# Six buffered halves of split weights, float32 work in half chunks, and a gate whose copies and silu are queued behind casts

## The chip, the cores and the metric

The kernel runs on one core of one Trainium2 chip. The metric is the device time of one execution in microseconds (us). The engines are TensorE (PE; its loads of weights are listed as PEld), VectorE (DVE), ScalarE (ACT), GpSimd (POOL) and SyncE (SP), which issues the DMA transfers.

## The reference

Two layers of an encoder for 256 positions of width 1024, in float32. Most of the time goes to the last part of the second layer, a mixture of experts:

```python
def moe_swiglu(xn, router, w_gu, w_down):
    logits = (xn @ router).astype(jnp.float32)
    top_v, top_i = lax.top_k(logits, TOP_K)          # 2 of 8
    w = jax.nn.softmax(top_v, axis=-1)
    ...
    for e in range(N_EXPERTS):
        out = out + comb[..., e:e + 1] * swiglu(xn, w_gu[e], w_down[e])
    return out

def swiglu(xn, w_gu, w_down):
    g, u = jnp.split(xn @ w_gu, 2, axis=-1)
    return (jax.nn.silu(g) * u) @ w_down
```

An expert has `w_gu` of 1024 x 7168 and `w_down` of 3584 x 1024. All eight experts' weights are read, 42 MiB each.

## The kernel before

The positions that chose an expert are gathered into at most 128 slots, and the weights stream past them. They come in chunks of 128 x 2048 float32 (1 MiB, one DMA each, issued by SyncE in the order of use). An expert is seven turns `j`. A turn has two chunks of gate weights, two of up weights, and, from the second turn on, the two chunks of down weights that belong to the turn before; the down chunks of the seventh turn follow after the loop.

TensorE does not multiply float32 at full rate here. A chunk is therefore split in two halves of 1024 columns, and each half in two parts: `hi`, a cast by ScalarE to the type float32r (L168), and `lo`, what VectorE's subtraction leaves of the chunk (L169). Four matmuls of a part use the 512 columns of four blocks of 128 rows. The pools `hi` and `lo` have `NPART = 4` buffers of half a chunk each.

Experts are sorted by how many positions chose them. In the positions 0, 1, 3, 5 and 7 of that order (wide) up to 128 slots are used, the activations are split too, and `moving` runs three matmuls per block: hi with hi, lo with hi, hi with lo. In the positions 2, 4 and 6 (narrow, `two` in the code) at most 64 slots are used; `hi` and `lo` of the activations stand side by side in one tile of 128 columns, and `narrow` runs two matmuls per block, one with each part of the weights. The two halves of the sum lie in the two halves of the partitions and are added afterwards. In narrow positions the last up chunk of a turn is not split: TensorE reads it as float32 (L1139), in eight records for the four blocks.

For a narrow turn the program's order is: gate product (`pg`); transposes of the h of the turn before (`to_rows`, L1172, with a cast at L1053 and a subtraction at L1054); up product (`pu`); then `gate`: two copies by ScalarE that swap the halves of `pg` (L1156, L1157), an addition by VectorE (L1158), silu by ScalarE (L1159), and `eh`, VectorE's product of silu and `pu` (L1163); then the two down products of the turn before.

The order on each engine is made ahead of time by a planner, which goes by program order and by its own estimate of when an instruction's operands and buffers are there. Each engine then works strictly in that order. `tc.issue_after(ins)` makes what is written under it come after `ins` on the same engine. `done[0]` is the last cast that `split` has written.

Chunk buffers come from two pools: 11 of the pool `raw`, and "spare" ones of the pool `big`, ten tiles of a chunk's size that also hold the tokens, the accumulator and other large tiles. `RING` says which chunk takes which kind, and `kinds.append(kinds[-(NRAW + 6)])` repeats it: 17 chunk buffers in all. SyncE issues a load when its buffer is free.

Of the kernel before, what the change touches and what calls it, by code (L numbers as in the profile page):

```python
# [25 lines left out]
F32 = mybir.dt.float32  # L26
F32R = mybir.dt.float32r
I32 = mybir.dt.int32
AF = mybir.ActivationFunctionType
# [3 lines left out]
P = 128  # L33
# [6 lines left out]
NE = 8  # L40
# [4 lines left out]
CH = 2048  # L45
# [4 lines left out]
HALF = CAP // 2  # L50
TCKW = dict(schedule_with_timeline_sim=True)
NCKW = dict(dynamic_dma_scratch_size=512)
NRAW = 11
NPART = 4
RING = "rrrrrrrrsssssrrrrrs"
P2_POOL = (0, 2, 4, 6)
NWARM = 10
NAHEAD = 13
# [23 lines left out]
def _build(ctx, tc, io, cap):  # L82
# [3 lines left out]
    rawp = ctx.enter_context(tc.tile_pool(name="rawp", bufs=NRAW))  # L86
# [3 lines left out]
    work = ctx.enter_context(tc.tile_pool(name="work", bufs=2))  # L90
    w2b, w1b = 4, 5
# [6 lines left out]
    V, S, G, PE = nc.vector, nc.scalar, nc.gpsimd, nc.tensor  # L98

    def f32(ap):  # L100
        return ap.bitcast(F32)
# [41 lines left out]
    def load(ap, n=CH, pieces=1, spare=False):  # L143
# [3 lines left out]
            nc.sync.dma_start(raw[:, sl], ap[:, sl])  # L147
        return raw

    done = []  # L150

    def split(raw, n=CH, pieces=2, apart=()):

        cut = (n // 2 + P - 1) // P * P
        parts = []
        for a, b in ((0, cut), (cut, n)):
            if len(parts) in apart:  # L160
                both = rawp.tile([P, CH], F32R, tag="raw", name="apart")
                hi, lo = both[:, :CH // 2], both[:, CH // 2:]
            else:
                hi = hip.tile([P, CH // 2], F32R, tag="hi", name="hi")
                lo = lop.tile([P, CH // 2], F32R, tag="lo", name="lo")
            step = (b - a) * 2 // pieces
            for i in range(0, b - a, step):
                done[:] = (S.copy(hi[:, i:i + step], raw[:, a + i:a + i + step]),  # L168
                           V.tensor_sub(lo[:, i:i + step], raw[:, a + i:a + i + step],  # L169
                                        f32(hi[:, i:i + step])))  # L170
            parts.append((hi, lo))

        def at(a, b):
            hi, lo = parts[a >= cut]
            o = cut if a >= cut else 0
            return hi[:, a - o:b - o], lo[:, a - o:b - o]
        return at

    class Early:
# [11 lines left out]

        def __call__(self, a, b):
            return self.hi[:, a:b], self.lo[:, a:b]

    def raw_tile(name, dt=F32):
        return rawp.tile([P, CH], dt, tag="raw", name=name)

    def raw_pair(name):
        return [raw_tile(name, F32R) for _ in range(2)]
# [355 lines left out]
    for g, w in enumerate(POOL_WINDOWS):  # L555
        left, right = w // 2, w - 1 - w // 2
        G.memset(invc[:, g, :], 1.0 / w)
        for t in list(range(left)) + list(range(T - right, T)):
            n = min(t + right, T - 1) + 1 - max(t - left, 0)
# [142 lines left out]
    ps = None  # L702
    for m in range(KD):
        if m % 2 == 0:
            ps = halves(acc_tile())
# [4 lines left out]
        for hf in range(2):  # L710
            w = split(load(io["ffn_down"][m, hf], half * P), half * P)
# [86 lines left out]
    last = conv31(KD - 1)  # L798
# [5 lines left out]
    ws = early[:2] + ws  # L804
# [134 lines left out]
    def fetch():  # L939
        n, (ap, pieces) = next(source)  # L940
        ahead.append(load(ap, pieces=pieces, spare=kinds[n] == "s"))
        kinds.append(kinds[-(NRAW + 6)])

    for _ in range(NAHEAD):
        fetch()
# [161 lines left out]
    xg = big_tile("xg", F32R)  # L1107
    ht = big_tile("ht", F32R)

    def whole_chunk():  # L1110
        if not ahead:
            fetch()
        return ahead.popleft()

    def chunk(pieces=2):
        return split(whole_chunk(), pieces=pieces)

    def narrow(ps, xs, ws, first, last):

        n = len(xs)  # L1120
        for part in range(2):
            for i, (x, w) in enumerate(zip(xs, ws)):
                ins = PE.matmul(ps, x, w[part], start=first and i == part == 0,  # L1123
                                stop=last and part == 1 and i == n - 1)
        return ins

    def expert(e, g, following):
        nonlocal fn
        py = out_tiles()
        two = e in NARROW  # L1130

        def gate_up(j, gu):
            pz = acc_tile("gu")
            for kh in range(2):
                xs = [xg[:, k * P:(k + 1) * P] for k in range(kh * 4, kh * 4 + 4)]
                if two and gu == kh == 1:
                    w = whole_chunk()
                    for kk in range(4):
                        PE.matmul(pz, f32(xs[kk]), w[:, kk * 512:(kk + 1) * 512],  # L1139
                                  start=False, stop=kk == 3)  # L1140
                    continue
                w = chunk()
                ws = [w(kk * 512, (kk + 1) * 512) for kk in range(4)]
                if two:
                    narrow(pz, xs, ws, kh == 0, kh == 1)
                    continue
                moving(pz, [(xg[:, k * P:(k + 1) * P], xg[:, D + k * P:D + (k + 1) * P])
                            for k in range(kh * 4, kh * 4 + 4)],
                       ws, kh == 0, kh == 1)
            return pz  # L1150

        def gate(pg, pu):
            sg = work.tile([P, 512], F32, tag="w2", name="esg", bufs=w2b)
            if two:

                S.copy(sg[:HALF], pg[HALF:])  # L1156
                S.copy(sg[HALF:], pg[:HALF])  # L1157
                V.tensor_add(sg, sg, pg)  # L1158
                S.activation(sg, sg, AF.Silu, scale=g.cw[:, 1:2])  # L1159
            else:  # L1160
                S.activation(sg, pg, AF.Silu, scale=g.cw[:, 1:2])
            h = work.tile([P, 512], F32, tag="w2", name="eh", bufs=w2b)
            V.scalar_tensor_tensor(h, pu, g.cw[:, 1:2], sg, op0=ALU.mult, op1=ALU.mult)  # L1163
            return h

        def to_rows(j, h):
            pt = tr_tile("ht")
            o = (j % 2) * D
            if two:

                for i in range(4):
                    PE.matmul(pt[:, i * HALF:(i + 1) * HALF], h[:, i * P:(i + 1) * P], both,  # L1172
                              start=True, stop=True)
                return side_by_side(ht[:, o:o + 512], pt[:, :4 * HALF])
            for i in range(4):
                PE.transpose(pt[:, i * P:(i + 1) * P], h[:, i * P:(i + 1) * P], ident)
            S.copy(ht[:, o:o + 512], pt)
            V.tensor_sub(ht[:, o + 512:o + D], pt, f32(ht[:, o:o + 512]))

        def down(j, n):  # L1180
            w = chunk(4 if e == NE - 1 and j == 6 else 2)
            o = (j % 2) * D
            if two:
                return narrow(py[n], [ht[:, o + f * P:o + (f + 1) * P] for f in range(4)],
                              [w(f * 512, (f + 1) * 512) for f in range(4)], j == 0, j == 6)
            return moving(py[n],
                   [(ht[:, o + f * P:o + (f + 1) * P], ht[:, o + 512 + f * P:o + 512 + (f + 1) * P])
                    for f in range(4)],
                   [w(f * 512, (f + 1) * 512) for f in range(4)], j == 0, j == 6)

        def weighted(n):
            src = py[n]
            hi, lo = (work.tile([P, 512], F32R, tag="w2", name=name, bufs=w2b) for name in ("yh", "yl"))
            S.activation(hi, src, AF.Copy, scale=g.cw[:, 0:1])
            done[:] = [V.scalar_tensor_tensor(lo, src, g.cw[:, 0:1], f32(hi),
                                              op0=ALU.mult, op1=ALU.subtract)]
            return hi, lo

        def scatter(n, y, tile=tr_tile):
            for t in range(2):  # L1200
                pz = tile("so")
                PE.matmul(pz, g.oT[:, t * P:(t + 1) * P], y[0], start=True, stop=False)
                PE.matmul(pz, g.oT[:, t * P:(t + 1) * P], y[1], start=False, stop=True)
                a = acc[:, t * D + n * 512:t * D + (n + 1) * 512]
                V.tensor_add(a, a, pz)  # L1205

        h = None
        for j in range(7):
            pg = gate_up(j, 0)
            if j:  # L1210
                to_rows(j - 1, h)
            pu = gate_up(j, 1)
            h = gate(pg, pu)
            if j:
                down(j - 1, 0)
                if j == 6:
                    to_rows(6, h)
                down(j - 1, 1)
            if following is not None and j in (3, 5):
                following.step(j)  # L1220
        if following is not None:
            following.rows()
        else:
            fn = big_tile("fn")
            nc.sync.dma_start(fn[:, :D], io["final_norm"].to_broadcast([P, D]))
        down(6, 0)
        y = weighted(0)
        last = down(6, 1)
# [276 lines left out]
```

## Time and profile before

| what | value |
| --- | --- |
| time, median of 3 runs | 1547.85 us (1547.59 to 1548.0) |
| profiled execution, its own time | 1547.42 us |
| its span, first to last instruction | 1545.7 us |
| experts, from the first gate matmul to the last scatter | 590.7 to 1532 us |
| wide expert, for instance | 943 to 1066 us |
| narrow experts | 832.5 to 943, 1066 to 1177, 1299 to 1408 us |

Times below are us from the start of the span unless marked ns. Everything before 590 us (the first layer, the convolution module and both attentions) is left as it is by the change, as is what follows the experts.

### The profile page before, as it was taken

The page shows a single profiled execution, that of the slowest core. Times are in us where ns is not written, and L with a number is a line of the kernel's source. Part 1 is how long each engine was busy: PE and PEld are TensorE (multiplying, and loading weights), DVE is VectorE, ACT ScalarE, POOL GpSimd, SP SyncE. Part 2 cuts the span into 40 slices and gives each one's busy share as a digit, 9 for nine tenths or more (in the row PEclk, how much of TensorE's full clock was granted, in tenths as well). Part 3 has the DMA queues.
Part 4 walks back from the last instruction along what each step waited for, and adds up shares of the span by engine and source line. Part 5 has one row for each costly group of instructions (what it writes and reads, how often), then busy time and mean ns, then how long its engine had stood idle before and what let it go on. Part 6 is the DMA issues. An engine that isn't in the chain of part 4 may idle for free.

```text
span 1545.7 us, 23643 instructions
## 1 busy us (share of the span) xinstructions
PE 1511.9 (98%) x8558; PEld 1294.3 (84%) x8558; DVE 1298.9 (84%) x1735; ACT 1052.1 (68%) x1381; POOL 148.1 (10%) x230
## 2 busy tenths in 40 slices
PE   8999999999999999999999999999999999999996
PEld 8899999999998998888888768888667888667885
DVE  7876677776898868999999989889889888889897
ACT  6555554455585647777777877777777777777775
POOL 4710100001394210000000000000000000000000
PEclk9999999999999999999999999999999999999998
DMA  9654454336536566998999999998999999999950
GB/s 370 269 191 164 142 186 166 120 113 236 188 134 244 174 264 221 371 377 334 373 366 342 397 422 412 381 375 331 403 402 376 367 361 343 408 392 382 364 191 30
DMA packets 65213, 451.42 MB, mean 292 GB/s; under 512 B 7360, under 2 KB 7488, under 8 KB 12480
## 3 DMA queue, kind: packets, MB, share of 16 engines
q1 hardware_dynamic: 65088, 449.83, 76.6%
q8 instruction: 69, 1.13, 0.3%
q14 instruction: 56, 0.46, 0.1%
HBM read 448.75 MB, written 1.05 MB: 291 GB/s over the span
## 4 chain that ended last, share of the span: by engine, by line
PE 82%; DVE 9%; POOL 3%; issue 3%; ACT 2%; DMA 1%; SPq 0%; DVEq 0%; POOLq 0%; ACTq 0%
PE gu L211 8%; PE gu L212 8%; PE gu L216 8%; PE acc L205 7%; PE acc L203 7%; PE acc L204 7%; DVE lo L169 6%; PE gu L1139 5%; PE gu L1123 4%; PE py L211 4%; PE py L216 4%; PE py L212 4%; PE py L1123 3%; POOL part L779 2%; PE gx L1042 1%
## 5 line engine op out<-in xcount | busy, mean ns | idle before, releaser
L169 DVE TENSOR_TENSOR lo<-raw,hi 128x1024 fp32r<-128x1024 f32 (+3 forms) x573 | 671.6, 1208 | 113.9 <-ACT hi L168 103.6
L168 ACT CAST hi<-raw 128x1024 fp32r<-128x1024 f32 (+3 forms) x573 | 565.4, 1030 | 212.9 <-PE acc L204 89.4
L169 DVE TENSOR_TENSOR lo<-spare,hi 128x1024 fp32r<-128x1024 f32 (+1 forms) x226 | 260.9, 1198 | 24.4 <-ACT hi L168 20.4
L168 ACT CAST hi<-spare 128x1024 fp32r<-128x1024 f32 (+1 forms) x226 | 221.5, 1035 | 23.6 <-PE gu L212 11.7
L211 PE MATMUL gu<-hi,xg 128*128 128x512 f32 x560 | 218.8, 391 | 0.0
L212 PE MATMUL gu<-hi,xg 128*128 128x512 f32 x560 | 218.3, 390 | 0.0
L216 PE MATMUL gu<-lo,xg 128*128 128x512 f32 x560 | 154.2, 391 | 0.6 <-DVE lo L169 0.6
L216 PEld LDWEIGHTS gu<-lo,xg 128*128 128x128 f32 x560 | 104.7, 188 | 23.9 <-DVE lo L169 1.9
L211 PEld LDWEIGHTS gu<-hi,xg 128*128 128x128 f32 x560 | 105.1, 188 | 22.2 <-ACT hi L168 0.2
L212 PEld LDWEIGHTS gu<-hi,xg 128*128 128x128 f32 x560 | 105.1, 188 | 21.8
L211 PE MATMUL py<-hi,ht 128*128 128x512 f32 x280 | 111.1, 398 | 0.0
L212 PE MATMUL py<-hi,ht 128*128 128x512 f32 x280 | 109.3, 390 | 0.0
L205 PE MATMUL acc<-a2h,lo 128*128 128x256 f32 x336 | 95.2, 283 | 0.0
L204 PE MATMUL acc<-a2l,hi 128*128 128x256 f32 x336 | 95.2, 283 | 0.0
L203 PE MATMUL acc<-a2h,hi 128*128 128x256 f32 x336 | 95.1, 283 | 0.0
L1401 POOL TENSOR_TENSOR fo<-accum,fn 128x512 f32<-128x512 f32 x2 | 2.5, 1272 | 948.9 <-DVE accum L1205 948.9
L1123 PE MATMUL gu<-lo,xg 128*128 128x512 f32 x252 | 80.4, 411 | 7.9 <-DVE lo L169 7.6
L216 PE MATMUL py<-lo,ht 128*128 128x512 f32 x280 | 84.0, 395 | 0.0
L1123 PE MATMUL gu<-hi,xg 128*128 128x512 f32 x252 | 71.3, 397 | 0.0
L1123 PEld LDWEIGHTS gu<-lo,xg 128*128 128x128 f32 x252 | 43.4, 188 | 31.5 <-DVE lo L169 25.2
L203 PEld LDWEIGHTS acc<-a2h,hi 128*128 128x128 f32 x336 | 64.5, 192 | 0.0
L205 PEld LDWEIGHTS acc<-a2h,lo 128*128 128x128 f32 x336 | 64.5, 192 | 0.0
(424 smaller groups left out, 3171.9 us busy)
## 6 DMA issues: line engine op xcount, KB each, us to landing
raw<-in_moe_gu SPq DMA_DIRECT2D x139, 1024.0 KB, 7.1
spare<-in_moe_gu SPq DMA_DIRECT2D x85, 1024.0 KB, 7.2
raw<-in_moe_down SPq DMA_DIRECT2D x78, 1024.0 KB, 7.4
spare<-in_moe_down SPq DMA_DIRECT2D x32, 1024.0 KB, 7.0
raw<-in_ffn_gu SPq DMA_DIRECT2D x22, 1024.0 KB, 4.8
raw<-in_pw SPq DMA_DIRECT2D x12, 1024.0 KB, 4.8
raw<-in_ffn_down SPq DMA_DIRECT2D x16, 704.0 KB, 4.1
raw<-in_wk SPq DMA_DIRECT2D x8, 1024.0 KB, 7.3
```

What stands on the lines that cost most here:

```text
L168: done[:] = (S.copy(hi[:, i:i + step], raw[:, a + i:a + i + step]), V.tensor_sub(lo[:, i:i + step], raw[:, a + i:a + i + step], f32(hi[:, ...
L169: V.tensor_sub(lo[:, i:i + step], raw[:, a + i:a + i + step], f32(hi[:, i:i + step])))
L203: PE.matmul(ps, a[0], b[0], start=first, stop=False)
L204: PE.matmul(ps, a[0], b[1], start=False, stop=False)
L205: PE.matmul(ps, a[1], b[0], start=False, stop=last)
L211: PE.matmul(ps, a[0], b[0], start=first and i == 0, stop=False)
L212: PE.matmul(ps, a[1], b[0], start=False, stop=False)
L216: ins = PE.matmul(ps, a[0], b[1], start=False, stop=last and i == n - 1)
L779: G.tensor_add(part, part, prod)
L1042: PE.matmul(px[:, kk * P:(kk + 1) * P], xt[:, t * D + d0:t * D + d0 + P], oh[:, t, :], start=t == 0, stop=t == 1)
L1123: ins = PE.matmul(ps, x, w[part], start=first and i == part == 0, stop=last and part == 1 and i == n - 1)
L1139: PE.matmul(pz, f32(xs[kk]), w[:, kk * 512:(kk + 1) * 512], start=False, stop=kk == 3)
```

## The change

- Every third half that is split gets its `hi` and `lo` in one tile of the pool `big` (`apart` in `split`), so six halves can be in work at once and no longer four. The number of spare chunk buffers falls from six to four (`NSPARE`), so the ring has 15 chunk buffers.
- In narrow positions no chunk is used whole any more. The second half of the first up chunk, and the second half of the second down chunk, stay float32; the last up chunk is split. `narrow` runs the matmuls of the float32 half after those of the split one.
- The copies and the addition of `gate` become `fold`. It is written in the middle of the up product, behind the cast of the first half of the first up chunk.
- In narrow turns the first down chunk of the turn before is split ahead of `gate`, and silu is queued behind the last cast of that chunk.

```diff
 NPART = 4
-RING = "rrrrrrrrsssssrrrrrs"
+NSPARE = 4
+NHALF = 6
+RING = "rrrrrrrrssssrrrrr"
...
         for a, b in ((0, cut), (cut, n)):
+            if len(parts) in whole:
+                parts.append(None)
+                continue
             if len(parts) in apart:
-                both = rawp.tile([P, CH], F32R, tag="raw", name="apart")
+                both = tile_of("apart", F32R)
                 hi, lo = both[:, :CH // 2], both[:, CH // 2:]
...
-        kinds.append(kinds[-(NRAW + 6)])
+        kinds.append(kinds[-(NRAW + NSPARE)])
...
-    def chunk(pieces=2):
-        return split(whole_chunk(), pieces=pieces)
+    def chunk(pieces=2, whole=()):
+        if not ahead:
+            fetch()
+        own = []
+        for i in range(2):
+            if i not in whole:
+                halves_split[0] += 1
+                if halves_split[0] % (NHALF // 2) == 0:
+                    own.append(i)
+        return split(ahead.popleft(), pieces=pieces, apart=own, whole=whole, tile_of=big_tile)
 
     def narrow(ps, xs, ws, first, last):
-        n = len(xs)
-        for part in range(2):
-            for i, (x, w) in enumerate(zip(xs, ws)):
-                ins = PE.matmul(ps, x, w[part], start=first and i == part == 0,
-                                stop=last and part == 1 and i == n - 1)
+        todo = [(x, w[part]) for part in range(2) for x, w in zip(xs, ws) if isinstance(w, tuple)]
+        todo += [(f32(x), w) for x, w in zip(xs, ws) if not isinstance(w, tuple)]
+        for i, (x, w) in enumerate(todo):
+            ins = PE.matmul(ps, x, w, start=first and i == 0, stop=last and i == len(todo) - 1)
...
-        def gate_up(j, gu):
+        def gate_up(j, gu, pg=None):
...
-                if two and gu == kh == 1:
-                    w = whole_chunk()
-                    for kk in range(4):
-                        PE.matmul(pz, f32(xs[kk]), w[:, kk * 512:(kk + 1) * 512],
-                                  start=False, stop=kk == 3)
-                    continue
-                w = chunk()
+                w = chunk(whole=(1,) if two and gu and kh == 0 else ())
                 ws = [w(kk * 512, (kk + 1) * 512) for kk in range(4)]
+                if two and gu and kh == 0:
+                    with tc.issue_after(done[0].ins):
+                        pg = fold(pg)
...
+        def fold(pg):
+            sg = work.tile([P, 512], F32, tag="w2", name="esg", bufs=w2b)
+            S.copy(sg[:HALF], pg[HALF:])
+            S.copy(sg[HALF:], pg[:HALF])
+            V.tensor_add(sg, sg, pg)
+            return sg
...
-            w = chunk(4 if e == NE - 1 and j == 6 else 2)
+            if w is None:
+                w = chunk(4 if e == NE - 1 and j == 6 else 2, (1,) if two and n else ())
...
-            pu = gate_up(j, 1)
-            h = gate(pg, pu)
+            pg, pu = gate_up(j, 1, pg)
+            w = chunk() if j and two else None
+            with tc.issue_after(done[0].ins) if two else nullcontext():
+                h = gate(pg, pu)
             if j:
-                down(j - 1, 0)
+                down(j - 1, 0, w)
```

## Rows read from the trace of the kernel before

**Rows 1.** The page, part 1: busy us of each engine, share of the span, instructions.
```profile
PE 1511.9 (98%) x8558; PEld 1294.3 (84%) x8558; DVE 1298.9 (84%) x1735; ACT 1052.1 (68%) x1381; POOL 148.1 (10%) x230
```

**Rows 2.** Stretches: start:end, length, busy us per engine, granted clock, DMA share, GB/s.
```profile
832.50:943.00 110.50, 109.65 (x474) 81.35 (x474) 101.32 (x108) 90.77 (x110) 0.00 (x0) 1.00 0.99 397
943.00:1066.00 123.00, 122.81 (x573) 101.88 (x572) 111.73 (x111) 93.01 (x104) 0.00 (x0) 1.00 0.98 377
1066.00:1177.00 111.00, 106.89 (x441) 73.57 (x440) 95.24 (x101) 82.82 (x102) 0.00 (x0) 1.00 0.97 388
...
1299.00:1408.00 109.00, 104.93 (x434) 71.99 (x433) 94.06 (x99) 81.34 (x100) 0.00 (x0) 1.00 0.98 388
```

**Rows 3.** Timeline of TensorE, float32 blocks: start, length, line, operands, records merged.
```profile
854.97 3.59 PE L1139 MATMUL gu<-raw,xg 128*128 128x512 f32 x8
...
909.48 3.59 PE L1139 MATMUL gu<-raw,xg 128*128 128x512 f32 x8
925.03 1.45 PE L1139 MATMUL gu<-raw,xg 128*128 128x512 f32 x3
...
1081.85 3.59 PE L1139 MATMUL gu<-raw,xg 128*128 128x512 f32 x8
...
1159.94 1.45 PE L1139 MATMUL gu<-spare,xg 128*128 128x512 f32 x3
```

**Rows 4.** Timeline of a short turn; in brackets idle time before and its releaser.
```profile
893.55 0.62 PE L1123 MATMUL gu<-hi,xg 128*128 128x512 f32 x2
894.00 1.07 PE L1123 MATMUL gu<-lo,xg 128*128 128x512 f32 x4
...
894.65 0.58 ACT L1156 COPY esg<-gu 64x512 f32<-64x512 f32 x1 [0.29 <-PE gu L1123]
...
895.85 1.99 ACT L168 CAST hi<-spare 128x1024 fp32r<-128x1024 f32 x2
...
897.75 0.72 ACT L1159 ACTIVATE esg<-esg,cw 128x512 f32<-128x512 f32 x1
...
903.92 0.37 ACT L1053 CAST ht<-ht 128x256 fp32r<-128x256 f32 x1 [0.65 <-PE ht L1172]
```

**Rows 5.** Timeline of a long turn.
```profile
1105.44 6.89 DVE L169 TENSOR_TENSOR lo<-raw,hi 128x1024 fp32r<-128x1024 f32 x6
...
1110.89 0.59 ACT L1156 COPY esg<-gu 64x512 f32<-64x512 f32 x1 [1.58 <-PE gu L1123]
...
1112.25 0.68 DVE L1158 TENSOR_TENSOR esg<-esg,gu 128x512 f32<-128x512 f32 x1
...
1112.96 0.72 ACT L1159 ACTIVATE esg<-esg,cw 128x512 f32<-128x512 f32 x1 [0.90 <-DVE esg L1158]
...
1114.65 1.23 DVE L169 TENSOR_TENSOR lo<-spare,hi 128x1024 fp32r<-128x1024 f32 x1 [1.72 <-ACT hi L168]
...
1116.60 0.75 DVE L1163 SCALAR_TENSOR_TENSOR eh<-gu,cw,esg 128x512 f32<-128x512 f32 x1 [0.72 <-PE gu L1139]
...
1117.79 1.00 PE L1172 MATMUL ht<-kept,eh 128*128 128x64 f32 x8
...
1118.83 0.37 ACT L1053 CAST ht<-ht 128x256 fp32r<-128x256 f32 x1 [1.36 <-PE ht L1172]
```

**Rows 6.** Waits from 1066 to 1177: us in total, times, longest.
```profile
PEld gu L1123 <- DVE lo L169: 11.5, 21, 0.8
```

**Rows 7.** Stretches of two short turns and of one long turn.
```profile
882.60:909.20 26.60, 26.60 (x115) 19.69 (x114) 25.06 (x27) 21.77 (x27) 0.00 (x0) 1.00 1.01 423
...
1101.00:1116.60 15.60, 14.74 (x57) 9.56 (x57) 13.12 (x13) 11.78 (x15) 0.00 (x0) 1.00 1.01 416
```

**Rows 8.** Waits of SyncE's queue from 590 to 1532.
```profile
SPq L147 <- DVE lo L169: 591.3, 262, 14.6
SPq L147 <- PE gu L1139: 76.7, 21, 5.0
```

**Rows 9.** DMA issues from 882 to 943: count, KB each, median us to landing.
```profile
spare<-in_moe_gu SPq DMA_DIRECT2D x7, 1024.0 KB, 15.2
```

More of the change, by code (lines that the diff above doesn't have):

```diff
@@ L148, in load, with raw_tile, split @@
         return raw
+    def raw_tile(name, dt=F32):
+        return rawp.tile([P, CH], dt, tag="raw", name=name)
     done = []
-    def split(raw, n=CH, pieces=2, apart=()):
+    def split(raw, n=CH, pieces=2, apart=(), whole=(), tile_of=raw_tile):
         cut = (n // 2 + P - 1) // P * P
@@ L173, in at @@
         def at(a, b):
+            if parts[a >= cut] is None:
+                return raw[:, a:b]
             hi, lo = parts[a >= cut]
@@ L193, in __call__ @@
             return self.hi[:, a:b], self.lo[:, a:b]
-    def raw_tile(name, dt=F32):
-        return rawp.tile([P, CH], dt, tag="raw", name=name)
     def raw_pair(name):
@@ L1108, in _build @@
     ht = big_tile("ht", F32R)
-    def whole_chunk():
+    halves_split = [0]
+    def chunk(pieces=2, whole=()):
         if not ahead:
             fetch()
-        return ahead.popleft()
-    def chunk(pieces=2):
-        return split(whole_chunk(), pieces=pieces)
-    def narrow(ps, xs, ws, first, last):
-        n = len(xs)
-        for part in range(2):
-            for i, (x, w) in enumerate(zip(xs, ws)):
-                ins = PE.matmul(ps, x, w[part], start=first and i == part == 0,
-                                stop=last and part == 1 and i == n - 1)
+        own = []
[5 more added lines that the diff above has]
+        return split(ahead.popleft(), pieces=pieces, apart=own, whole=whole, tile_of=big_tile)
+    def narrow(ps, xs, ws, first, last):
+        todo = [(x, w[part]) for part in range(2) for x, w in zip(xs, ws) if isinstance(w, tuple)]
+        todo += [(f32(x), w) for x, w in zip(xs, ws) if not isinstance(w, tuple)]
+        for i, (x, w) in enumerate(todo):
+            ins = PE.matmul(ps, x, w, start=first and i == 0, stop=last and i == len(todo) - 1)
         return ins
@@ L1149, in gate_up @@
                        ws, kh == 0, kh == 1)
-            return pz
-        def gate(pg, pu):
[L1153 to L1161, printed above, removed]
+            return (pg, pz) if gu else pz
+        def fold(pg):
[4 more added lines that the diff above has]
+            return sg
+        def gate(pg, pu):
+            sg = pg if two else work.tile([P, 512], F32, tag="w2", name="esg", bufs=w2b)
+            S.activation(sg, pg, AF.Silu, scale=g.cw[:, 1:2])
             h = work.tile([P, 512], F32, tag="w2", name="eh", bufs=w2b)
@@ L1178, in to_rows, with down @@
             V.tensor_sub(ht[:, o + 512:o + D], pt, f32(ht[:, o:o + 512]))
-        def down(j, n):
-            w = chunk(4 if e == NE - 1 and j == 6 else 2)
+        def down(j, n, w=None):
+            if w is None:
+                w = chunk(4 if e == NE - 1 and j == 6 else 2, (1,) if two and n else ())
             o = (j % 2) * D
```

## The prediction

> **What bounds the kernel now.** I first read the page's busy shares: TensorE is busy 98% of the span, VectorE 84%, ScalarE 68% [rows 1]. An average cannot say where a change pays, so the second view is the table of stretches, cut at the experts [rows 2]. In a wide expert (943 to 1066) TensorE is busy 122.81 of 123.00 us: feeding it better can win 0.2 us there. In the narrow experts at 1066 and 1299 it is busy 106.89 of 111 and 104.93 of 109 us, so something keeps it waiting; the narrow expert at 832 loses only 0.85 us.
>
> The third view is the timeline of TensorE. Each narrow turn runs one whole float32 chunk (L1139), so the starts of that block are a ruler [rows 3]. The five turns from 1081.85 to 1159.94 take 78.09 us, 15.62 each. In the narrow expert at 832 four turns from 854.97 to 909.48 take 54.51 us, 13.63 each, and the fifth, to 925.03, takes 15.55. The expert at 1299 loses 4.07 us of busy TensorE where that at 1066 loses 4.11 [rows 2]; I count five turns of 15.62 for it too. So there are eleven long turns (171.7 us) and four short turns (54.5): 226.2 us, 15.08 in the mean. The shorter first turns and the ends of the experts I leave as they are.
>
> The work of TensorE in a turn follows from runs of matmuls in a short turn [rows 4]: four take 1.07 us and two 0.62, so one more costs 0.225, and 40 cost 9.0. Eight records of the float32 chunk take 3.59 us and three 1.45 [rows 3], so one is 0.43 and eight 3.42. The eight small ones that transpose and fold h take 1.00 [rows 5]. Sum: 13.4 us. A short turn is bound by TensorE, a long one loses 2.2 us.
>
> What it waits for is in the waits of 1066 to 1177: loads of `lo` weights, held by VectorE's subtraction at L169, 11.5 us in 21 waits [rows 6]. Yet VectorE has only 13.12 us of work in a long turn and ScalarE 11.78 [rows 7]; both are late, not full. The timeline of one long turn says why [rows 5]. ScalarE comes to the copy of the gate's sum (L1156) and waits 1.58 us for TensorE; VectorE's addition (L1158) starts at 1112.25, behind six subtractions; the silu (L1159) waits 0.90 for it; and the casts of the down weights stand behind the silu. So VectorE has nothing to subtract for 1.72 us. Then `eh` (L1163) waits 0.72 for the float32 block. That is 2.44 us of idle VectorE, and 13.12 + 2.44 = 15.56, the turn. In the short turn [rows 4] two casts (at 895.85) go between copies and silu, and the silu waits for nothing.
>
> **The change, part by part.** *Silu behind the casts of the next down chunk.* This makes the order of the short turns the rule. The addition no longer holds a cast up, so the 1.72 us goes. The silu is queued behind two casts (1.99 us together [rows 4]), and `eh`, the transposes of h and their cast come later by that; who waits is the down product of h, a turn away.
>
> *Float32 halves.* Before, a turn split ten halves and ran one chunk whole; now it splits ten and runs two halves whole: four records of 0.43 us twice instead of eight once. That is nothing on TensorE, nor on ScalarE and VectorE. What moves is that the last up chunk is split, so `eh` waits for its `lo` matmuls and not for a 3.59 us block; standing behind the casts of down, it finds them done. The 0.72 us goes. Entering and leaving a float32 block twice a turn I price at nothing: a short turn of 13.63 leaves only 0.2 us over the sum of 13.4 for the edges of its one block. That 0.2 is the other bound, 3 us in fifteen turns.
>
> *Copies behind one cast.* The new order allows the copies after the first half of the first up chunk. Here is the one new wait: behind the copies stand all later casts, and behind those the subtractions. Rows 5 price it. Six subtractions take 6.89 us and one 1.23, so one more costs 1.13. The fourth of six, the gate's last, ends at about 1110.07 (1105.44 + 6.89 less two at 1.13); the copy starts at 1110.89, 0.82 later, and two copies take 1.18. With **one** cast ahead, VectorE subtracts that half (1.13 us), waits until 2.00 for the copies, adds (0.68), and gets the next half after another cast of 1.0, at 3.00: idle 0.87 + 0.32 = 1.19 us, a turn of 14.3. With **two** ahead it subtracts until 2.26, adds until 2.94 and idles 0.06: the turn is TensorE's 13.4. Which it will be the trace does not show. In rows 5 two are ahead, and that is natural: the gate's sum is ready a subtraction of 1.13 and 0.82 us after its last cast, the length of two casts. I take two as the rule and one as the exception: 13.8.
>
> *Six halves.* Every third half gets a buffer of its own, so ScalarE can run six halves ahead and not four. It costs two chunk buffers, 17 down to 15. SyncE's waits are nearly all for buffers, 591.3 us on VectorE and 76.7 us, in 21 waits, on the float32 block [rows 8]; it will now wait twice a turn on such a block, and behind it wait only later loads. What covers this is the ring: at 13.8/6 = 2.3 us a chunk, 15 buffers are 34.5 us from issue to reuse, and landing takes 15.2 us in the slowest group of a time when the queues are full [rows 9]. Some 19 us stay, so I price it at nothing; without this cover the transfers set the turn (below). In wide experts more halves gain at most the 0.2 us above.
>
> **Sum.** Eleven long turns: 11 x 13.8 - 171.7 = -19.9 us. Four short turns: 4 x 13.8 - 54.5 = +0.7. Together -19.2, against the profiled execution's 1547.42: 1528.2. That execution is 0.43 under the median of 1547.85, so 1528.7, say **1529**. With every turn at 13.4 it is 226.2 - 201.0 = 25.2 less, 1522.6; at 14.3 it is 11.7 less, 1536.1; 0.1 us of a turn is 1.5 us of time.
>
> **A rule on the transfers.** While the short turns ran, the queues moved 423 GB/s at a share of 1.01 [rows 7]: full. Six chunks of 1.049 MB at that rate take 14.9 us, more than the turn I forecast. The forecast rests on the ring: over seven turns of 13.8 the queue falls 7 x (14.9 - 13.8) = 8 us behind, which the 19 us of cover hold, and the next wide expert makes it good.
>
> The Trainium skill, Perfetto Trace Analysis, section Roofline, gives 358 GB/s as a core's share of the memory when its neighbour runs too, and some 435 GB/s, that of sixteen DMA engines, as the ceiling of a core alone. The trace agrees with the second, at 423. Estimated from that page's 435, a turn bound by transfers would be 14.5 us, and the time about 1539.
>
> **Rivals.** (1) *The copies hold ScalarE*: they stand behind one cast in every turn, and TensorE, which may have the transposes of h (1.00 us [rows 5]) before the gate's last matmuls, comes to their sum that much later. The turn is 14.3 + 1.0 = 15.3, fifteen turns 229.5 us, the time 1551: slower. It decides from a turn of 15.08 on, with TensorE 0.8 us behind. For it: 1.58 us are already waited at this copy [rows 5]; against it: six buffers let other casts go first. (2) *ScalarE becomes the bound*: its 11.78 us of work, the 1.58 at the copy and 1.36 at the cast of h [rows 5] all stay, 14.7 a turn: 5.7 us less, 1542. Against it: in the short turn these waits are 0.29 and 0.65 [rows 4]. (3) *Transfers become the bound*, the cover being gone: 14.9 a turn, 1545. Against it: four turns of 13.63 ran while the queues were full. (4) *The stall moves and stays as large*: `eh`, later by two casts, makes TensorE wait at the transposes, and the turns stay at 15.1: 1548.
>
> **Chances.** Turns of 13.4 to 13.9 (1522.6 to 1530.2): 0.50. Turns to 14.3, one cast ahead in many of them (to 1536.1): 0.20. Rival 2: 0.10, up to 1544. Rival 3: 0.04, half of it within 0.2%. Rival 1: 0.12, a sixth of it within 0.2%. Rival 4: 0.04, no change. A difference under 0.2%, 3.1 us here, is about what a measurement cannot tell from none. Faster: 0.50 + 0.20 + 0.10 + 0.02 = 0.82; same: 0.02 + 0.02 + 0.04 = 0.08; slower: 0.10. The range from 1522.5 to 1545 holds the first two, rival 2 and most of rival 3, about 0.83; the first two alone are 0.70, so it is not narrower.
>
> **What would show it.** Starts of the up chunk's float32 half some 13.8 us apart in all three narrow experts; no subtraction (L169) in them that waits over 1 us for a cast; a silu that waits for nothing; waits of TensorE's loads on `lo` under a third of the 11.5 us; wide experts unchanged to 0.5 us; some 420 GB/s in narrow stretches. The prediction is wrong if the copies wait over 1.5 us each turn with an idle VectorE behind them, or if casts wait for landing chunks.

## The result and the profile after

The changed kernel takes 1584.42 us, median of 4 (1584.05 to 1585.16), beside 1547.92 (1547.59 to 1548.09) for the kernel before: a ratio of 1.0237, 95% interval 1.0219 to 1.0254. It is 36.5 us slower; the forecast was 18.9 us faster, and the range ended at 1545.

The first view is again the page's busy time of each engine, the line that answers to [rows 1].

```profile
PE 1534.2 (97%) x8558; PEld 1292.4 (82%) x8558; DVE 1302.1 (82%) x1735; ACT 1043.1 (66%) x1381; POOL 148.1 (9%) x230
```

The instructions are the same in number, and ScalarE and VectorE have as much work as before. TensorE is busy 22.3 us longer with the same matmuls, but its busy time holds waiting too: in the kernel before, the third expert takes 101.65 us of it for 440 matmuls and the fifth 106.59 for 441, both at a granted clock of 1.00. So nearly all of the time is waiting. The profiled execution has a span of 1583.4 us, 37.7 more than before. I cut it at the first matmul of each expert: the eight experts took 123.2, 123.9, 102.6, 124.2, 110.7, 124.2, 110.9 and 122.7 us before; they take 131.0, 126.9, 116.3, 124.4, 113.9, 127.2, 115.0 and 125.1 after. Of the 37.4 us, 16.4 are lost in wide experts, which the forecast left unchanged, and 21.0 in narrow ones, which it saw 19.2 shorter. The table of stretches, cut at those points, has the first five (start:end, length, busy us of PE, PEld, DVE, ACT and POOL, granted clock, DMA share, GB/s):

```profile
591.00:722.00 131.00, 127.12 (x584) 104.57 (x582) 112.80 (x145) 94.49 (x107) 0.00 (x0) 0.97 0.63 241
722.00:848.90 126.90, 125.21 (x583) 103.73 (x582) 109.89 (x108) 89.62 (x103) 0.00 (x0) 1.00 0.84 339
848.90:965.30 116.40, 110.50 (x436) 72.01 (x434) 98.74 (x103) 85.05 (x104) 0.00 (x0) 0.99 0.95 391
965.30:1089.60 124.30, 124.30 (x580) 103.26 (x579) 111.20 (x111) 91.59 (x104) 0.00 (x0) 1.00 0.91 370
1089.60:1203.50 113.90, 109.30 (x438) 72.08 (x438) 98.06 (x102) 83.69 (x103) 0.00 (x0) 1.00 0.95 388
```

In the two narrow experts shown TensorE now idles 5.9 and 4.6 us, more than in [rows 2]. The DMA share of the first expert is 0.63, of the second 0.84; no transfer is the limit there.

The granted clock of 0.97 in the first expert is one stretch, 638.0 to 644.8 us, at the lower of TensorE's two levels (0.50 of full speed, 1.2 GHz). In the 8 us before it TensorE was busy for 5.77 us only. As an estimate, 6.8 us at half speed cost at most 3.4 of the 7.8 us that this expert lost. The kernel before has no such stretch in its experts.

The second view is the timeline of the narrow expert of 1089.60. The starts of `eh` (L1174), VectorE's last step of a turn, are the ruler now, and in brackets stands the idle time before an instruction with what ended it:

```profile
1128.20 0.75 DVE L1174 SCALAR_TENSOR_TENSOR eh<-gu,cw,esg 128x512 f32<-128x512 f32 x1
...
1130.41 0.37 ACT L1061 CAST ht<-ht 128x256 fp32r<-128x256 f32 x1 [2.38 <-PE ht L1183]
...
1130.82 0.42 DVE L1062 TENSOR_TENSOR ht<-ht 128x256 fp32r<-128x256 f32 x1 [0.74 <-ACT ht L1061]
...
1131.76 1.23 DVE L178 TENSOR_TENSOR lo<-raw,hi 128x1024 fp32r<-128x1024 f32 x1 [0.52 <-ACT hi L177]
...
1134.47 1.05 ACT L177 CAST apart<-raw 128x1024 fp32r<-128x1024 f32 x1
...
1137.21 0.58 ACT L1165 COPY esg<-gu 64x512 f32<-64x512 f32 x1 [1.69 <-PE gu L1136]
...
1138.41 0.69 DVE L1167 TENSOR_TENSOR esg<-esg,gu 128x512 f32<-128x512 f32 x1 [0.89 <-ACT esg L1166]
...
1139.48 2.36 DVE L178 TENSOR_TENSOR lo<-raw,hi 128x1024 fp32r<-128x1024 f32 x2 [0.38 <-ACT hi L177]
...
1142.20 0.72 ACT L1172 ACTIVATE esg<-esg,cw 128x512 f32<-128x512 f32 x1
...
1144.03 0.75 DVE L1174 SCALAR_TENSOR_TENSOR eh<-gu,cw,esg 128x512 f32<-128x512 f32 x1
```

The turn is 1144.03 - 1128.20 = 15.83 us. One cast stands ahead of the copies (1134.47), as in the unlucky case of the forecast, and it does so in every turn: ScalarE waits 1.69 for the gate's sum, and VectorE idles 0.89 + 0.38. The silu (1142.20) and `eh` wait for nothing, as forecast. But a wait that the forecast had not counted stands at the start of the turn: the cast of h (L1061) waits 2.38 for the transposes, the next casts stand behind it, and VectorE idles 0.74 + 0.52. The row of the stretch gives the rest:

```profile
1128.18:1144.03 15.85, 15.06 (x56) 9.45 (x56) 13.32 (x14) 11.73 (x14) 0.00 (x0) 1.00 1.01 420
```

13.32 busy and 0.74 + 0.52 + 0.89 + 0.38 = 2.53 idle are 15.85.

The third view is that of SyncE's waits from 590 to 1570 (us in total, times, longest), which answers to [rows 8]:

```profile
SPq L149 <- DVE apart L178: 433.7, 77, 16.5
SPq L149 <- PE gu L224: 101.5, 35, 6.5
SPq L149 <- DMA raw<-in_moe_gu: 97.4, 46, 3.5
SPq L149 <- DMA raw<-in_moe_down: 45.2, 21, 3.6
SPq L149 <- PE py L224: 41.1, 13, 7.1
```

L224 is the third matmul of `moving`, in wide experts. Before, a load there waited for VectorE's subtraction, which is the last to read a chunk. Now 48 loads wait 142.6 us for TensorE: the chunk's slot was last used not by a chunk but by an `apart` tile, which is free only when the matmuls have read it. The pool `big` has both kinds of tile, its slots go round, and so loads get slots that `apart` tiles leave. All later loads stand behind the waiting one. SyncE also waits 142.6 us, 67 times, for an earlier load to land, which it does not do in the kernel before. The longest hole is in the first expert, in the timeline of SyncE:

```profile
602.30 4.56 SPq L149 DMA_DIRECT2D raw<-in_moe_down  x2
616.59 0.33 SPq L149 DMA_DIRECT2D raw<-in_moe_gu  x1
635.85 0.33 SPq L149 DMA_DIRECT2D spare<-in_moe_gu  x1
```

For 19 us no load is issued. The page's list of DMA issues (count, KB each, median us to landing) says that most loads, once issued, now take twice as long, because they go out in clumps:

```profile
raw<-in_moe_gu SPq DMA_DIRECT2D x171, 1024.0 KB, 15.6
raw<-in_moe_down SPq DMA_DIRECT2D x75, 1024.0 KB, 17.6
```

On the page of before these are 7.1 and 7.4. That the clumps are the reason is only argued; that the held slots below bring back 7.2 and 7.4 is measured.

A late load costs time only if a cast waits for it. From the list of all waits of the same stretch:

```profile
PEld ht L1187 <- DVE eh L1174: 7.6, 6, 1.3
...
ACT apart L177 <- DMA spare<-in_moe_down: 2.4, 1, 2.4
...
ACT apart L177 <- DMA raw<-in_moe_gu: 0.8, 2, 0.4
```

All casts together wait 4.0 us, in 6 waits, for a chunk to land, 3.2 of it in the first expert. So late chunks by themselves do not make up the loss; the experiments come back to this.

### The profile page after: what moved, and what is told of

It is laid out like the page before. It is cut to its first block, busy times and chain, and to the rows that moved or that the text cites. A ratio compares the mean times of both kernels' runs of the same rounds, so it can differ in the third digit from the quotient of the medians.

```text
span 1583.4 us, 23038 instructions
## 1 busy us (share of the span) xinstructions
PE 1534.2 (97%) x8558; PEld 1292.4 (82%) x8558; DVE 1302.1 (82%) x1735; ACT 1043.1 (66%) x1381; POOL 148.1 (9%) x230
## 4 chain that ended last, share of the span: by engine, by line
PE 73%; DVE 13%; ACT 5%; issue 3%; DMA 3%; POOL 3%; SPq 0%; POOLq 0%; DVEq 0%; ACTq 0%
PE gu L219 8%; PE gu L220 8%; PE gu L224 8%; DVE lo L178 7%; PE acc L213 7%; PE acc L212 7%; PE acc L211 6%; PE py L220 4%; PE py L224 4%; PE py L219 4%; DVE apart L178 3%; PE py L1136 3%; PE gu L1136 2%; DMA raw<-in_moe_gu 2%; POOL part L787 2%
## 5 line engine op out<-in xcount | busy, mean ns | idle before, releaser
L178 DVE TENSOR_TENSOR lo<-raw,hi 128x1024 fp32r<-128x1024 f32 (+2 forms) x476 | 561.7, 1202 | 93.1 <-ACT hi L177 89.6
L177 ACT CAST hi<-raw 128x1024 fp32r<-128x1024 f32 (+2 forms) x476 | 474.6, 1023 | 185.4 <-PE acc L212 90.1
L178 DVE TENSOR_TENSOR apart<-raw,apart 128x1024 fp32r<-128x1024 f32 (+1 forms) x157 | 188.8, 1206 | 18.0 <-ACT apart L177 17.9
L177 ACT CAST apart<-raw 128x1024 fp32r<-128x1024 f32 (+1 forms) x157 | 162.3, 1037 | 4.9 <-DVE lo L178 2.4
L219 PE MATMUL gu<-hi,xg 128*128 128x512 f32 x368 | 144.9, 394 | 0.0
L220 PE MATMUL gu<-hi,xg 128*128 128x512 f32 x368 | 143.7, 390 | 0.0
L178 DVE TENSOR_TENSOR lo<-spare,hi 128x1024 fp32r<-128x1024 f32 x111 | 132.8, 1220 | 8.9 <-ACT hi L177 6.6
L177 ACT CAST hi<-spare 128x1024 fp32r<-128x1024 f32 x111 | 112.8, 1050 | 3.8 <-PE py L220 2.4
L224 PE MATMUL gu<-lo,xg 128*128 128x512 f32 x368 | 108.2, 391 | 0.0
L219 PEld LDWEIGHTS gu<-hi,xg 128*128 128x128 f32 x368 | 69.1, 188 | 15.0 <-issue 0.5
L220 PEld LDWEIGHTS gu<-hi,xg 128*128 128x128 f32 x368 | 69.2, 188 | 14.7 <-issue 0.5
L224 PEld LDWEIGHTS gu<-lo,xg 128*128 128x128 f32 x368 | 68.8, 188 | 14.2
L219 PE MATMUL gu<-apart,xg 128*128 128x512 f32 x192 | 75.6, 394 | 0.2 <-ACT apart L177 0.2
L220 PE MATMUL gu<-apart,xg 128*128 128x512 f32 x192 | 74.9, 390 | 0.0
```

The costliest lines, as they stand in the source:

```text
L219: PE.matmul(ps, a[0], b[0], start=first and i == 0, stop=False)
L220: PE.matmul(ps, a[1], b[0], start=False, stop=False)
L224: ins = PE.matmul(ps, a[0], b[1], start=False, stop=last and i == n - 1)
```

## The experiments

Each run is compared with runs of the kernel before on the same chip. Where two runs are set against each other, the chips can differ; the medians of the kernel before on these chips are 1547.92 to 1548.54. "Held slots" are an edit of mine: two `apart` tiles are taken from the pool `big` once and used in turn, so no load ever gets their slots. Two theories stood at the start: the buffers cost it (the third halves take slots from loads), or the order costs it (copies behind one cast).

### The buffers alone, and the order alone

e1_six_alone is the kernel before with the change's buffers and nothing else; e2_order_four is the change without them.

```diff
# e1, from the kernel before
+RING = "rrrrrrrrssssrrrrr"
-        return split(whole_chunk(), pieces=pieces)
+        return split(whole_chunk(), pieces=pieces, apart=own, tile_of=big_tile)
# e2, from the changed kernel
+NSPARE = 6
+RING = "rrrrrrrrsssssrrrrrs"
-                if halves_split[0] % (NHALF // 2) == 0:
-                    own.append(i)
```

> Only the buffers of the change: every third half in a tile of its own from the pool big, 15 chunk buffers; narrow turns as before. Theory A, the buffers cost the wide experts and the start (in the changed kernel the first expert took 131.0 us for 123.2, the second 126.9, the sixth 127.2, the eighth 125.1): about 16 us more, 1564, and SyncE's loads wait for TensorE's reads of an apart tile. Theory B, the loss is in the narrow order alone: 1548, within 3 us.

> The change without its buffers: four halves, 17 chunk buffers, no apart tiles; float32 halves, early copies and late silu as changed. Theory A: the buffers' 16 us go, 1568, with narrow turns still at 15.8 and wide experts at 123 to 124. Theory B: 1584 stays, since all of it lies in the narrow order. A third possibility, that six halves made the planner put the copies early: turns fall to 13.5 to 14.3 and the time to 1530 to 1540.

e1: 1581.79 us beside 1548.08, ratio 1.0219 (1.0202 to 1.0236). e2: 1559.83, ratio 1.0078 (1.0061 to 1.0094). Both theories hold in part, and the buffers weigh three times as much: +33.7 and +11.8. Neither size was as expected (1564 for e1, 1568 for e2). The sum of 45.5 is more than the change's 36.5, so they overlap. In e1 the waits of the changed kernel are all there, with a turn written as before:

```profile
SPq L149 <- DVE apart L171: 435.6, 80, 16.6
SPq L149 <- DMA raw<-in_moe_gu: 98.9, 45, 3.5
SPq L149 <- PE gu L218: 89.2, 35, 6.7
```

Its experts (129.7, 126.9, 114.8, 124.3, 112.9, 126.8, 114.2, 125.2) have the changed kernel's losses too: 6.5 in the first, 2.5 to 3.1 in three wide ones, 12.1 in the third. The narrow turns of the third had been short, and now are 15.55 as in the other two narrow experts; no cast there waits for a chunk to land. In e2 all wide experts are within 0.4 us of before, and the turns are 15.84 in the fifth and seventh expert; the third takes 106.2 us, with turns of 11.9 to 16.0 behind its first.

### The two parts of the order

```diff
# e3, from e2: copies behind the first cast of the last up chunk
-                if two and gu and kh == 0:
+                if two and gu and kh == 1:
# e4, from e2: copies as in the change, silu not queued behind casts
-            w = chunk() if j and two else None
-            with tc.issue_after(done[0].ins) if two else nullcontext():
-                h = gate(pg, pu)
+            w = None
+            h = gate(pg, pu)
```

> As the run with four halves, but the copies and the addition are written behind the casts of the second up chunk, so three casts stand ahead of them and not one. Theory C, the copies behind one cast cost 1.3 us of idle VectorE a turn (0.89 + 0.38 in the changed kernel): turns 14.5, about 20 us under the run with the copies early, near 1548. Theory D, the late silu and the wait of ScalarE at the cast of h (2.38 us a turn) set the turn: it stays at 15.8 and the time at 1568.

> As the run with four halves, copies early, but silu and eh are written ahead of the split of the next down chunk, as before the change. Theory D, the late silu: the wait at the cast of h falls from 2.4 to 1.4 us, VectorE's idle 0.74 + 0.52 goes, turns 14.6, near 1548. Theory C, the early copies: turns stay at 15.5 or more, 1565.

e3: 1544.67, ratio 0.9977 (0.9967 to 0.9987). e4: 1551.5, ratio 1.0023 (1.0013 to 1.0033). Later copies give back 15.2 us of e2, and the order turns from a loss to a gain. All of that lies in the fifth and seventh expert. The turns of the third are the same in e2, e3 and e4 but for one: 15.97, 17.06 and 15.94 us, and there the granted clock is at its lower level for 3.4, 6.8 and 3.4 us. What else holds the third expert, no run here shows. Taking back the silu gives 8.3, which the forecast had not seen: queued behind the casts, with the copies early, silu cost time. The timeline of a turn in e3 says why.

```profile
1108.32 0.37 ACT L1061 CAST ht<-ht 128x256 fp32r<-128x256 f32 x1 [2.84 <-PE ht L1181]
...
1108.73 0.42 DVE L1062 TENSOR_TENSOR ht<-ht 128x256 fp32r<-128x256 f32 x1 [0.98 <-ACT ht L1061]
...
1109.67 8.04 DVE L178 TENSOR_TENSOR lo<-raw,hi 128x1024 fp32r<-128x1024 f32 x7 [0.52 <-ACT hi L177]
...
1115.35 0.58 ACT L1163 COPY esg<-gu 64x512 f32<-64x512 f32 x1
```

The copy waits for nothing; what is left is the cast of h, 2.84 us, with 0.98 + 0.52 of idle VectorE behind it, and 13.10 + 1.50 = 14.60 is the turn. The later silu makes `eh` late, and `eh` the transposes. In e4, where `eh` comes earlier, the cast of h waits 1.22 and no VectorE waits behind it; its turns are 15.15, from the copies (2.15 on ScalarE, 1.36 + 0.38 on VectorE).

### Buffers with slots of their own, and the smaller ring

```diff
# e5, from e1 (e9: the same, from the changed kernel)
+        def own_tile(name, dt): # takes two tiles from big_tile, then uses them in turn
-        return split(whole_chunk(), pieces=pieces, apart=own, tile_of=big_tile)
+        return split(whole_chunk(), pieces=pieces, apart=own, tile_of=own_tile)
# e6, from the kernel before
-RING = "rrrrrrrrsssssrrrrrs"
+RING = "rrrrrrrrssssrrrrr"
```

> The buffers alone, as in the run with six halves alone, but the two tiles for every third half are held for the whole stage and used in turn, so no chunk load ever takes a slot that such a tile has left. Theory E, sharing of slots in the pool big costs the 33 us (SyncE waited 89 + 35 us for TensorE's reads): the time falls back to 1548, within 4 us. Theory F, it is the smaller ring of 15 chunk buffers: it stays at 1570 to 1582.

> The kernel before with a ring of 15 chunk buffers, four spare ones and not six, nothing else; four halves. Theory E: 1548, within 3 us, since 15 buffers cover a landing of 7 us. Theory F: 1570 to 1582.

> The whole change with one thing mended: the two tiles for every third half are held for the whole stage, so no chunk load takes a slot from them. Theory E, shared slots and the narrow order add up: the run with four halves (1559.8) less the 1.2 us that held slots gave by themselves, 1558 to 1560. If six halves let more casts go ahead of the copies, as the prediction had it: turns of 13.4 to 14.3 and a time of 1530 to 1540.

e5: 1546.85 beside 1548.1, ratio 0.9987 (0.9977 to 0.9997). e6: 1546.01, ratio 0.9985 (0.9975 to 0.9994). e9: 1554.9 beside 1548.54, ratio 1.0043 (1.0026 to 1.006). A ring of 15 costs nothing, nor does it cost anything to have six halves; 34.9 us of e1 lie between slots that loads share and slots that they don't. In the whole change it is 29.5. With held slots the change is still 6.4 us slower than the kernel before, where the forecast had 18.9 less: the narrow turns of its fifth and seventh expert stay at 15.84, as in e2, and that part is the order's. In e5 the first waits of SyncE are on VectorE again, the third is the float32 block of [rows 8], and none is on L218:

```profile
SPq L149 <- DVE lo L171: 386.8, 169, 6.7
SPq L149 <- DVE apart L171: 216.2, 93, 16.5
SPq L149 <- PE gu L1156: 62.9, 19, 6.3
```

### The cast of h behind the gate's casts

The call of `to_rows` gets the same treatment as the copies: it comes after the first cast of the gate's last chunk.

```diff
# e7, from e3; e10, from e2; e8, from the kernel before with silu behind casts
-                to_rows(j - 1, h)
+                with tc.issue_after(done[0].ins) if two else nullcontext():
+                    to_rows(j - 1, h)
```

> Four halves, float32 halves, copies behind the casts of the second up chunk, silu behind the casts of down, and now also the cast of h (L1061) queued behind the casts of the next gate chunks. If the wait of ScalarE at that cast (2.84 us, VectorE idle for 0.98 + 0.52) is what is left between 13.1 and 14.6: turns of 13.4 to 13.6 and a time near 1525. If the stall moves to TensorE's down product: no gain over 1544.7.

> The kernel before with its whole float32 chunk, copies where they were, and only two orders added: silu behind the casts of the next down chunk, cast of h behind the casts of the gate. If the order alone matters and the float32 halves do nothing: turns of 13.4 to 13.6, about 1527. If eh still waits 0.72 us for the whole block: turns of 14.1, about 1537.

> Four halves and the order of the change, copies early, with only the cast of h queued behind the casts of the next gate chunks. It prices the copies alone: if the idle times add up, 13.12 + 0.89 + 0.38 = 14.4 a turn in the narrow experts at the fifth and seventh place, where 15.84 were measured, so 1542. If ScalarE's 1.7 us at the copies fall away with the other wait: 13.4 a turn, 1531. If nothing is won: 1559.8.

e7: 1536.74 beside 1548.1, ratio 0.9923 (0.9907 to 0.994), 7.9 us under e3. Three turns of e7, and after them the one turn of an expert that stays at 15.84:

```profile
1091.10:1130.80 39.70, 39.70 (x166) 28.98 (x165) 39.13 (x41) 35.20 (x43) 0.00 (x0) 1.00 1.01 413
```

```profile
1134.06 0.37 ACT L1100 CAST oT<-ot 128x256 fp32r<-128x256 f32 x1 [3.06 <-PE ot L1098]
```

TensorE is busy in all of the 39.70 us: 13.2 us a turn, the bound that the forecast had put at 13.4. In the long turn a cast for the next expert's selection holds ScalarE. The turns came as expected, the time (near 1525) did not: two long turns cost some 5 us, and the third expert takes 107.3 us, as in e3, for 102.6 in the kernel before.

e8 keeps the whole float32 chunk: 1537.57, ratio 0.9929 (0.9913 to 0.9946). Its turns are 14.49, because `eh` waits for the whole block, twice the 0.72 of [rows 5]:

```profile
1113.33 0.75 DVE L1165 SCALAR_TENSOR_TENSOR eh<-gu,cw,esg 128x512 f32<-128x512 f32 x1 [1.47 <-PE gu L1139]
```

Yet its total is only 0.8 us over e7: its third expert takes 101.0 us (e7: 107.3) and makes up for the 3.5 and 3.9 us by which the other two are longer. Part of that is the clock: e7 has 6.8 us at the lower level in its third expert, e8 none. So the half chunks are worth 1.3 us in a pinned turn (all of VectorE's idle time in a turn of e8 is that wait, 13.03 + 1.47 = 14.50), and about nothing over the whole of these two kernels, which also differ in the place of the copies.

e10 was a miss. Copies behind one cast, with the cast of h out of the way, should have given turns of 14.4; they are 14.94, and the time is 1552.73 beside 1548.54, ratio 1.0027 (1.0016 to 1.0038).

```profile
1115.62 0.58 ACT L1163 COPY esg<-gu 64x512 f32<-64x512 f32 x1 [2.16 <-PE gu L1134]
1116.83 0.69 DVE L1165 TENSOR_TENSOR esg<-esg,gu 128x512 f32<-128x512 f32 x1 [1.44 <-ACT esg L1164]
```

With the casts ahead of it earlier, the copy waits longer, 2.16 and not 1.69, and VectorE idles 1.44 + 0.38 = 1.82. Taking one wait out of ScalarE's queue lengthens the next, so the two waits of the changed kernel don't simply add up.

### The last long turn, and all parts together

```diff
# e11, from e7: the next expert's step goes behind the same cast
+                    if two and following is not None and j in (4, 6):
+                        following.step(j - 1)
# e12: e11 with six halves in held slots and the ring of 15
# e13: e12, but the slots shared with loads as in the change (tile_of=big_tile)
# e14: e11 with the ring of 15
```

> As the run with the cast of h behind (1536.7), and the cast of the next expert's transposed selection, at which ScalarE waited 3.06 us in one turn of each of two narrow experts (15.84 us for 13.2), also moved behind the casts of the next gate chunks. If that wait is the reason of these two turns: 5 us less, near 1531.5. If transfers were the reason (413 GB/s in those turns): 1536.7.

> All together: copies late, silu, cast of h and cast of the selection behind casts, float32 halves, and six halves with two tiles held for them and 15 chunk buffers. If six halves help where the order no longer stalls: 1 to 2 us under the run with four halves, near 1530. If they do nothing: the same within 1.5 us. If they change the planner's order for the worse: over 1536.

> The run with all together (1533.2), but the tiles for every third half again come and go in the pool big, so chunk loads and such tiles share slots, as in the change. If sharing costs through the chip's late loads, it costs the same 30 to 34 us under any order: 1563 to 1567, with casts that wait for landing chunks. If it costs through the order that is written ahead of time, the narrow experts, whose order is now mostly pinned, keep their 102 to 104 us, and only the wide ones and the first lose some 15: 1548, and no cast waits for a chunk.

> As the run with copies late and the casts of h and of the selection behind casts (1536.7, four halves), with 15 chunk buffers and not 17. If the 3.5 us that the run with six held halves gained came of six halves: 1536.7, within 1.5 us. If they came of the shorter ring, which by itself gave 2.1 us: 1533 to 1534.5.

e11: 1536.74 beside 1548.54, ratio 0.9925 (0.9908 to 0.9941): no gain. The long turn moved to the next place (15.36), where VectorE waits 2.24 us for the selection's matmul (L1103). e14: 1537.91 beside 1548.31, ratio 0.9936 (0.992 to 0.9953): the ring does nothing here either. e12: **1533.2** beside 1548.54, ratio 0.9897 (0.9881 to 0.9914), the best of all. Held halves are worth 3.5 us over e11 and 4.7 over e14; the interval of each ratio is 2.6 us to either side, so that they help is likely, by how much is not measured well. The profile of e14 has 6.8 us at the lower clock in the third expert, those of e11 and e12 have 3.4, and that was 1.1 us in the turn of e3 and e2 above.

e13: 1564.5 beside 1548.31, ratio 1.0107 (1.009 to 1.0124). With all other lines as in e12, the sharing costs 31.3 us. Stretches of three narrow turns, first of e12 and then of e13:

```profile
1101.90:1142.20 40.30, 40.30 (x169) 29.61 (x168) 39.35 (x41) 34.67 (x42) 0.00 (x0) 1.00 1.02 423
```

```profile
1118.20:1162.90 44.70, 43.30 (x168) 28.84 (x168) 39.87 (x41) 36.04 (x43) 0.00 (x0) 1.00 1.01 422
```

Both move 422 to 423 GB/s, at a DMA share of 1.01 to 1.02: the queues are full. In e12 a turn takes 13.4 all the same: loads fall behind by 1.5 us a turn, and the ring holds it. In e13 a turn takes 14.9, six chunks at that rate: the ring no longer runs ahead, and the casts wait for chunks to land, in the list of waits of e13 from 590 to 1570:

```profile
ACT apart L177 <- DMA raw<-in_moe_gu: 12.1, 18, 1.4
ACT hi L177 <- DMA raw<-in_moe_gu: 10.6, 17, 1.4
ACT hi L177 <- DMA spare<-in_moe_gu: 5.7, 7, 2.4
```

e12 has no such wait. In e13 these waits are 32.0 us in all, 28.7 of them in the narrow experts, which take 108.7, 108.9 and 109.1 us (e12: 103.9, 101.6, 102.2). This is the first theory, late loads, and it accounts for up to 19.0 us.

The second theory, the order that is written ahead of time, has the rest. The wide experts of e13 (129.6, 127.0, 127.2, 125.1, and 124.4 unchanged) lose as much as in the change, with 3.3 us of waits for a landing among them. In the first and the second expert the instructions of ScalarE and VectorE stand in one and the same order in the change, e1 and e13, and in one other order in e5, e9 and e12. In the second expert's later turns, for instance, VectorE makes its part of `ht` three subtractions behind `eh` with shared slots, and nine behind it with held slots. With shared slots `eh` is late for TensorE's transposes (`PEld ht` on `DVE eh`, 7.6 us in 6 waits, the same in e13, e1 and the change; none in e12), in turns of 17.9 and 18.6 where the kernel before has 16.8 and 17.5. No cast of the second expert waits for a landing in any of the three, so its 3 us are the order's alone.

In the change itself casts waited 4.0 us for landings, and in e1 2.5; narrow turns of 15.83 are longer than the 14.9 that six chunks need. Most of the 29.5 and 34.9 us there went through the order, then, and not through chunks that landed late. How the planner comes to that order, no run here shows; the slots are all that differs in the source.

## Why the prediction was wrong

- *Six halves*, "I price it at nothing", is **the step that failed**: by itself it turns the sign. It is not all, since without it the change still loses 6.4 us (e9) through the next two steps. That step asked whether 15 buffers are enough, and they are (e6, e14: no loss). It did not ask which slots the third halves' tiles take. They go round in the pool `big` with the chunks, so loads wait for TensorE's last read of an `apart` tile, every later load stands behind, and the planner writes another order of work for ScalarE and VectorE. Measured: 29.5 us (the change against e9), 31.3 (e13 against e12), 34.9 (e1 against e5). Waits of casts for landing chunks are 4.0 us in the change, and 32.0 in e13, nearly all in narrow experts. Counting transfers and buffers, as the forecast did, could not find the rest. The four short turns, which the sum had at +0.7 us, show it most: their expert, the third, is 13.7 us longer in the change and 1.1 in e9. The row that could have said so was not in the trace of before, but the diff had it: `tile_of=big_tile`.
- *Copies behind one cast*: the working was right, the choice wrong. One cast ahead was priced at 0.87 + 0.32 = 1.19 us of idle VectorE, and it is 0.89 + 0.38 = 1.27. I took two casts "as the rule and one as the exception"; it is one in all turns. In [rows 5] the program has the copies behind all casts of the up product, and the planner put two ahead; the change writes them behind the first, and the planner left it at that. e3, with a later place, gains 15.2 us over e2.
- *Silu behind casts*: the 1.72 us of idle VectorE did go, as did the silu's wait. "Who waits is the down product of h, a turn away" was wrong: the first to wait is ScalarE itself, at the cast of h, 2.1 to 2.8 us, and behind it VectorE for 1.0 to 1.5. This was rival 4's mechanism (a later `eh`), at another place than the one it named. With it, and with the copies early, the silu costs 8.3 us more than it gives (e2 against e4); without it the order pays (e7).
- *Float32 halves*: `eh` waits for nothing, as forecast. What the whole block costs in a pinned turn is 1.3 us (14.49 against 13.2), not 0.72; over the experts this did not show, since the kernel with the whole chunk has a shorter third expert.
- The bounds: TensorE's turn of 13.4 is 13.2 measured. The edges of the float32 blocks cost nothing.
- Rival 1 (copies hold ScalarE, 15.3, 1551) came nearest: e2, the order without the buffers, has turns of 15.84 and a time of 1559.8. Its mechanism was right in part: it had the wait at the copies, and not the one at the cast of h. Rival 3 (transfers, 14.9) is what the narrow turns of e13 show, once the order no longer hides it: the "19 us of cover" hold only while the slots are not shared.
- Of the signs that were named: the copies wait over 1.5 us with an idle VectorE behind them, as "wrong if" had it; wide experts moved by 2.4 to 7.8 us, four in five, where 0.5 was said; TensorE's waits on `lo` and `apart` in the expert at 1089.60 are 13.3 us, not a third of 11.5.

The rule of the Trainium skill, Perfetto Trace Analysis, section Roofline, that was weighed ahead (435 GB/s as the ceiling of a core alone) stands: the trace agrees at 422 to 423 GB/s, and the turn that was estimated from it as 14.5 us is 14.9 in e13.

## What to carry to other kernels

When a change gives a tile a buffer, look at which pool's slots it takes and who frees them: a load queued for a slot that a matmul reads last waits for TensorE, and all loads behind it wait too. Where a planner writes the order, look also at how the order changed: most of the loss here was in it, and a busy share or a queue does not show that. A tile with a different last reader gets slots of its own. When a step is queued behind others, follow its result to the next instruction on the same in-order queue, not only to the product that needs it in the end: the cast that stood in the queue before the others cost more than the stall that was removed.

## What was not expected of the hardware

- TensorE ran three narrow turns with no idle time, at 13.2 us each in e7 and 13.4 in e12, while the queues moved 413 and 423 GB/s, less than six chunks a turn need at that pace; a ring of 15 chunks carried this through a whole narrow expert with no cast waiting for a landing (e12).
- Loads waited for TensorE 48 times, 3 us in the mean and 7.1 at most, in a kernel whose transfers have room on average (the DMA share is 0.63 to 0.91 in the first, second and fourth expert of the changed kernel), and yet casts waited only 4.0 us for a landing.
- Behind a hole in TensorE's work in the first expert of the changed kernel (5.77 us busy of 8) the granted clock stood at 0.50 for 6.8 us, so the hole cost more than its own length. In the third expert, runs with 6.8 us at that level have one turn of 17.0 to 17.1 us, and e2, e4 and e11, with 3.4 us, one of 15.9 to 16.0.
